# The second tile of a 31-tap convolution goes from VectorE to GpSimd, and the norm behind it runs beside the local attention

## The chip, the cores and the metric

One core of a Trainium2 chip runs the whole program. The metric is the time of one execution on the device in microseconds (us). The engines of the core are TensorE (PE; its weight loads are PEld), VectorE (DVE), ScalarE (ACT), GpSimd (POOL) and SyncE (SP), which issues the DMAs. Each engine works through its own queue strictly in order.

## The reference

Two layers of a transformer-like trunk in float32 over 512 latent tokens and 256 context tokens, width 1024. Each layer is a feed-forward block, a mixer of four parallel groups of 256 channels, and a second feed-forward block. The change is in the mixer's fourth group, the conformer convolution, and in when its norm runs:

```python
def conformer_conv_mix(z, w_conv, b_conv, g_ln, b_ln):
    a, gt = jnp.split(z, 2, axis=-1)
    u = a * jax.nn.sigmoid(gt)
    u = dw_conv(u, w_conv) + b_conv                 # 31 taps along the tokens, one weight per channel
    return jax.nn.silu(layer_norm(u, g_ln, b_ln))   # mean and variance over the 256 channels
```

The other three groups are a latent attention (4 heads, all tokens), a short gated convolution of 3 taps, and a local attention over windows of 128 tokens plus the context. All four read one input projection (`w_in`) of the normed tokens, and their outputs go through one output projection. Layer 0 computes all 768 tokens; in layer 1 the context is not needed behind its keys and values, so the convolution has 512 tokens there.

## The kernel before, in words

Activations lie with channels on the 128 partitions and tokens along the free dimension. TensorE multiplies float32 numbers that are split into a rounded high part and a rest, in three products (`mm3`, L168). Each weight tile of 128x1024 is loaded into one of four buffers `raw` (`load`, L158), taken round robin, and split in two halves of 512 columns into `wh` (ScalarE, L139) and `wl` (VectorE, L140).

`mixer` goes through these stages for each layer.

1. Two pairs of projections give the convolution's input `u`, two tiles of 128 channels (L725 writes them). Between latent and context tokens and at both ends lie 15 zero columns, so one instruction covers all tokens: 783 columns in layer 0, 512 in layer 1. `gap_conv` then makes each output tile `y` with 31 instructions: the middle tap with the bias (L651), and 30 of the form y = u shifted * w + y (L653). Both tiles run on VectorE. They are recorded at a priority of -1000 (`P_CONV`), so that the scheduler places them, when the program is built, where it expects VectorE to be free.
2. Projections of the local attention's queries, keys and values follow, with their rotations (L620 to L623) and copies for the products (L1006, L1014).
3. Local attention: per unit (`Window`, 12 units in layer 0, 8 in layer 1) scores on TensorE (L841 to L849), maximum, exponential and sum, and then GpSimd multiplies the probabilities by the reciprocal of the sum (L869). TensorE transposes them (L628 in `transposed`), and multiplies them by the values (L792, L793). The loop over `units` runs the softmax of unit i, the transposes of unit i - 1 and the products of unit i - 2. Between these it takes steps of the generator `others` (function `more`), which holds the projections of the short convolution and of the latent attention, eight steps of weights each. Their sums go to the PSUM tile `pmod` and a spare one.
4. Latent attention: the same loop goes on with 8 or 16 units of `Latent`. Here steps 4 to 7 (`CN`) each advance the generator `conformer_norm`: sums over the channels by products with a matrix of ones (L758), the subtraction of the mean (L762), the squares (L767), their sums and inverse root, the multiplication (L772), Silu with gain and shift (L775) and the split for the output projection. In this stage the buffers `raw[2]` and `raw[3]` also take weights of the modulation (L182), which a second generator, `filler`, works off.

The scheduler fixes the order of each engine's instructions when the program is built. At run time an engine waits for what its next instruction needs, and nothing behind it may pass.

Of the kernel before, what the change touches and what calls it, by code (L numbers as in the profile page):

```python
# [13 lines left out]
ALU = mybir.AluOpType  # L14
AX = mybir.AxisListType

P = 128
D = 1024
KD = D // P
# [12 lines left out]
CF_K = 31  # L32
# [14 lines left out]

class K:
    N_RAW, N_MRAW, N_W = 4, 2, 5
    CN = (4, 5, 6, 7)  # L50

    FFN_MODS = (0, range(2, 6)), (1, range(0, 4)), (1, range(4, 6)), (1, ())
    MIX_MODS = range(6, 9)
# [591 lines left out]
    def gap_conv(self, y, u, w, bias, n):  # L645
# [3 lines left out]
        for j in [mid] + [j for j in range(CF_K) if j != mid]:  # L649
            if j == mid:  # L650
                nc.vector.tensor_scalar(out=y[:, :n], in0=u[:, j:j + n], scalar1=w[:, j:j + 1], scalar2=bias, op0=ALU.mult, op1=ALU.add)  # L651
            else:
                nc.vector.scalar_tensor_tensor(out=y[:, :n], in0=u[:, j:j + n], scalar=w[:, j:j + 1], in1=y[:, :n], op0=ALU.mult, op1=ALU.add)  # L653


    def mixer(self, l, n, st):

        nc = self.nc
# [6 lines left out]
        nq = n // P  # L665
# [44 lines left out]
        dd = []  # L710
        us = []
        gap = self.GAP

        places = [(a, b, a + i * gap) for i, (a, b) in enumerate(segs)]
        for i in range(2):
            u = self.wide.popleft()
# [8 lines left out]
                    nc.vector.tensor_tensor(out=v[:, c - a:e - a], in0=ps, in1=v[:, c - a:e - a], op=ALU.mult)  # L725
            us.append(u)

        with self.rise(self.P_CONV):
            for i in range(2):
                y = self.wide.popleft()  # L730
                a, b, p = places[-1]
                self.gap_conv(y, us[i], self.vcol(l, "wcf", i * CF_K, CF_K), self.vcol(l, "bcf", i), p + b - a)
                dd.append(y)

        wq = []
# [15 lines left out]
            nc.scalar.activation(wv[:, a:b], ps, AF.Copy)  # L751

        def conformer_norm():
            self.give(*(u[:, :TOK] for u in us))
            pm = self.turn(self.dbl)
            for i, y in enumerate(dd):
                for a, b, p in places:
                    nc.tensor.matmul(pm[:, a:b], self.ones, y[:, p:p + b - a], start=i == 0, stop=i == 1)  # L758
            zs = [self.S(), self.S()]
            for y, z in zip(dd, zs):  # L760
                for a, b, p in places:
                    nc.vector.scalar_tensor_tensor(out=z[:, a:b], in0=pm[:, a:b], scalar=-1.0 / 256, in1=y[:, p:p + b - a], op0=ALU.mult, op1=ALU.add)  # L762
            self.give(*(y[:, :TOK] for y in dd))
            yield
            sqs = [self.S(), self.S()]
            for z, sq in zip(zs, sqs):
                nc.scalar.activation(sq[:, :n], z[:, :n], AF.Square)  # L767
            yield
            rl = self.inv_rms(self.turn(self.dbl), [(sq, P) for sq in sqs], n, 1.0 / 256)
            self.give(*sqs)  # L770
            for z in zs:
                nc.vector.tensor_tensor(out=z[:, :n], in0=z[:, :n], in1=rl[:, :n], op=ALU.mult)  # L772
            yield
            for i, z in enumerate(zs):
                nc.scalar.activation(z[:, :n], z[:, :n], AF.Silu, scale=self.vcol(l, "gln", i), bias=self.vcol(l, "bln", i))  # L775
            for j, t in zip((6, 7), zs):
                out(j, t)
            yield


        po = self.one
# [33 lines left out]
        so, _ = VEC["sink"]  # L815
# [207 lines left out]
        def out(i, t):  # L1023
            o[i] = self.split_new(t[:, :n], n)
            self.give(t)
# [16 lines left out]
        def others():  # L1042

            def short(i):
                t = self.turn(temps)
                for a, b, ps in (yield from slow(T_SC + 2 + i, n)):
                    nc.scalar.activation(t[:, a:b], ps[:, :b - a], AF.Copy)
                for a, b, ps in (yield from slow(T_SC + 4 + i, n)):
                    nc.vector.tensor_tensor(out=t[:, a:b], in0=ps[:, :b - a], in1=t[:, a:b], op=ALU.mult)
                cv = self.S()  # L1050
                self.dw_conv(cv, t, self.vcol(l, "wsc", i * SC_K, SC_K), SC_K, segs)
                for a, b, ps in (yield from slow(T_SC + i, n)):
                    nc.vector.tensor_tensor(out=cv[:, a:b], in0=ps[:, :b - a], in1=cv[:, a:b], op=ALU.mult)
                ob.append(cv)

            temps = deque(t[:, :TOK] for t in self.mraw)
            yield from short(0)

            pk = yield from slow(T_KV, TOK)
            ckv, sq = self.S(), self.turn(temps)  # L1060
            for a, b, ps in pk:
                nc.scalar.activation(ckv[:, a:b], ps[:, :b - a], AF.Copy)
                nc.scalar.activation(sq[:, a:b], ps[:, :b - a], AF.Square)
            for j in range(6):
                nc.tensor.matmul(spare[:, 256 + j:257 + j], sq[:, j * P:(j + 1) * P], self.ones[:, :1], start=True, stop=True)
            self.rsqrt(self.rc, spare[:, 256:262], 1.0 / 128)
            for a, b, ps in pk:
                self.spread(ps, self.rc[:, a // P:b // P])
                nc.vector.scalar_tensor_tensor(out=ckv[:, a:b], in0=ckv[:, a:b], scalar=self.vcol(l, "gkv"), in1=ps[:, :b - a], op0=ALU.mult, op1=ALU.mult)

            pq = yield from slow(T_QA, n)
            lat["kv"] = self.split_new(ckv, TOK)
            self.give(ckv)
            qa, sqa = self.S(), self.turn(temps)
            for a, b, ps in pq:
                nc.scalar.activation(sqa[:, a:b], ps[:, :b - a], AF.Square)
                nc.scalar.activation(qa[:, a:b], ps[:, :b - a], AF.Copy, scale=self.vcol(l, "gq", 0))
            lat["qa"] = self.split_new(qa[:, :n], n)
            self.give(qa)
            qw = query_weights(256)  # L1080
            pq = yield from slow(T_QB, TOK, 96)
            qb, sqb = self.S(), self.turn(temps)
            for a, b, ps in pq:
                if a < n:
                    nc.scalar.activation(sqb[lower, a:b], ps[lower, :b - a], AF.Square)
                    nc.scalar.activation(qb[lower, a:b], ps[lower, :b - a], AF.Copy, scale=self.vcol(l, "gq", 1)[lower])
                nc.scalar.activation(qb[64:96, a:b], ps[64:96, :b - a], AF.Copy)
            pr = spare[:, 256:]
            for t in range(nq):
                c = slice(t * P, (t + 1) * P)  # L1090
                nc.tensor.matmul(pr[:, 2 * t:2 * t + 2], sqa[:, c], self.ones[:, :2], start=True, stop=False)
                nc.tensor.matmul(pr[:, 2 * t:2 * t + 2], sqb[lower, c], self.ones[lower, :2], start=False, stop=True)
            rq = lat["rq"] = self.rq[l][:, :2 * nq]
            self.rsqrt(rq, pr[:, :2 * nq], 1.0 / 192)
            nc.vector.tensor_scalar(out=rq, in0=rq, scalar1=96 ** -0.5, scalar2=None, op0=ALU.mult)

            mqb = lat["qb"] = self.R()
            nc.scalar.activation(mqb[lower, :n], qb[lower, :n], AF.Copy)
            nc.vector.tensor_tensor(out=mqb[upper, :n], in0=qb[lower, :n], in1=mqb[lower, :n].bitcast(F32), op=ALU.subtract)
            self.rope(qb, 64, 96, self.cos_m, self.sin_m, self.mask_m)  # L1100
            lat["kr"] = qb

            q = lat["rot"] = self.S()
            parts = [(0, SEQ, self.mod_ps[:, :SEQ])] + ([(SEQ, n, spare[:, :n - SEQ])] if n > SEQ else [])
            mla_query(parts, 0, *qw)
            for a, b, ps in parts:
                nc.scalar.activation(q[:, a:b], ps, AF.Copy)
            self.rope(q, 0, P, self.cos_m, self.sin_m, self.mask_m, self.turn(temps))
            yield from short(1)

        units = [Window(t, kv) for kv in range(2) for t in range(nq)]
# [5 lines left out]
        cuts.close()  # L1117
        quad, spare = self.psum(cuts, 1, 1536)[0], self.psum(cuts, 1, 512)[0]
        lt, lv = self.LAGS
        cn, rest, done, total = conformer_norm(), others(), 0, 9 * KD  # L1120

        def more(share):

# [5 lines left out]
        for i in range(len(units) + lv):  # L1129
            j = i - nw  # L1130
            if j == -1:
                qw, kw = query_weights(), kv_weights()
            if j == 0:
                more(1)
                for _ in rest:
                    pass
                for t in (*x, wqs[1], wks[1]):
                    self.give(*t)
                cuts.close()
                self.dbl = self.psum(cuts, 2, 1024)  # L1140
                mraw = self.mraw
                self.mraw = deque(mraw + deque([self.raw[2], self.raw[3]]))
                self.filler = self.mod_parts(l, self.MIX_MODS)
                rot.extend(self.split_new(lat["rot"][:, :n], n))
                mla_queries(0, *qw)
                mla_keys(0, kw)
                self.give(lat["kr"], lat["rot"])
# [22 lines left out]
            if j == lv - 1:  # L1170
                self.give(*wvs)
            if j in self.CN:
                next(cn, None)
            if 0 <= j < 4:
                k, t = ((4, oc[0]), (2, ob[0]), (3, ob[1]), (5, oc[-1]))[j]
                out(k, t)
# [1 line left out]
                out(0, oa[0])  # L1178
            if j >= 0:
                self.fill(2)  # L1180
        for _ in cn:
            pass
        self.rest()
        self.mraw = mraw
        out(1, oa[1])
# [260 lines left out]
```

## Time and profile before

| | |
|---|---|
| median of 3 runs | 2645.79 us (2644.46 to 2647.66) |
| profiled execution | 2646.68 us, span of its instructions 2644.9 us |
| granted TensorE clock, mean | 0.987 |
| busy: TensorE, VectorE, ScalarE, GpSimd | 2573.0, 2173.6, 1131.2, 76.2 us |
| mixer of layer 0, local attention | about 640 to 770 us |
| mixer of layer 1, local attention | about 2032 to 2148 us |

Times are counted from the start of the span. A busy share is an average over stages with different limits, so the stretches are shown one by one below. In a line of the timeline or of a group, "[0.69 <-POOL f L869]" or the part behind the bar is the idle time of the engine before it and what ended it. Tiles go by the program's names, without buffer numbers: `f` are the mixer's float32 tiles (the convolution's inputs and outputs and the probabilities among them), `r` its rounded ones, `sm` small statistics, `ps`, `pmod` and `pone` PSUM tiles, `vec` the per-channel constants (the taps among them).

### The profile page before, as it was taken

The page shows a single profiled execution, that of the slowest core. Times are in us where ns is not written, and L with a number is a line of the kernel's source. Part 1 is how long each engine was busy: PE and PEld are TensorE (multiplying, and loading weights), DVE is VectorE, ACT ScalarE, POOL GpSimd, SP SyncE. Part 2 cuts the span into 40 slices and gives each one's busy share as a digit, 9 for nine tenths or more (in the row PEclk, how much of TensorE's full clock was granted, in tenths as well). Part 3 has the DMA queues.
Part 4 walks back from the last instruction along what each step waited for, and adds up shares of the span by engine and source line. Part 5 has one row for each costly group of instructions (what it writes and reads, how often), then busy time and mean ns, then how long its engine had stood idle before and what let it go on. Part 6 is the DMA issues. An engine that isn't in the chain of part 4 may idle for free.

```text
span 2644.9 us, 39614 instructions
## 1 busy us (share of the span) xinstructions
PE 2573.0 (97%) x15361; PEld 2430.6 (92%) x15361; DVE 2173.6 (82%) x4188; ACT 1131.2 (43%) x2118; POOL 76.2 (3%) x98
## 2 busy tenths in 40 slices
PE   7999999999998999999999999999999999999998
PEld 5999999987876999999999999999998776989998
DVE  5999987779877499999997778677679885788887
ACT  5333333444567343333324433234344565544444
POOL 0000000000212000000000000000000111000000
PEclk9999999999999999999999999999999999999999
DMA  7334332221134242344433112222121144323332
GB/s 279 125 103 130 116 99 64 80 72 34 39 124 136 64 152 88 105 136 144 125 115 96 48 60 65 68 64 80 58 85 60 43 128 129 122 85 96 96 101 76
DMA packets 78702, 257.24 MB, mean 97 GB/s; under 512 B 8753, under 2 KB 14385, under 8 KB 77873
## 3 DMA queue, kind: packets, MB, share of 16 engines
q1 hardware_dynamic: 78512, 254.70, 30.3%
q8 instruction: 120, 1.97, 0.3%
q14 instruction: 70, 0.57, 0.1%
HBM read 252.57 MB, written 2.10 MB: 96 GB/s over the span
## 4 chain that ended last, share of the span: by engine, by line
PE 65%; DVE 6%; ACT 2%; DMA 1%; issue 1%; POOL 0%; SPq 0%; DVEq 0%; ACTq 0%; POOLq 0%
PE ps L168 48%; PE pmod L168 7%; PE pone L168 5%; DVE f L653 1%; PE ps L628 1%; PE pmod L185 1%; DVE wl L140 1%; DMA raw<-in_w_mod 1%; PE pone L792 1%; DMA raw<-in_w_gu 1%; DVE r L140 1%; PE pone L793 1%; DVE f L140 0%; DVE sm L907 0%; DVE sm L855 0%
## 5 line engine op out<-in xcount | busy, mean ns | idle before, releaser
L168 PE MATMUL ps<-x,wh 128*128 128x384 f32 (+1 forms) x2888 | 703.2, 328 | 0.0
L168 PEld LDWEIGHTS ps<-x,wh 128*128 128x128 f32 x2888 | 510.8, 188 | 0.1
L168 PE MATMUL ps<-x,wl 128*128 128x384 f32 (+1 forms) x1444 | 473.1, 328 | 0.0
L139 ACT ACTIVATE wh<-raw 128x512 fp32r<-128x512 f32 (+1 forms) x439 | 275.1, 628 | 445.5 <-PE ps L168 264.2
L140 DVE TENSOR_TENSOR wl<-raw,wh 128x512 fp32r<-128x512 f32 (+1 forms) x439 | 302.0, 690 | 81.6 <-ACT wh L139 75.4
L168 PE MATMUL ps<-t,wh 128*128 128x384 f32 (+2 forms) x1408 | 364.9, 341 | 0.3 <-DVE t L140 0.3
L139 ACT ACTIVATE wh<-t 128x512 fp32r<-128x512 f32 x217 | 135.8, 629 | 328.6 <-PE ps L168 157.6
L168 PEld LDWEIGHTS ps<-x,wl 128*128 128x128 f32 x1444 | 271.2, 188 | 0.1
L323 DVE SCALAR_TENSOR_TENSOR h<-ps,hg,h 128x128 f32<-128x128 f32 (+3 forms) x376 | 174.4, 508 | 111.5 <-PE ps L168 109.9
L168 PE MATMUL ps<-r,wh 128*128 128x512 f32 (+3 forms) x1070 | 262.1, 337 | 0.4 <-DVE r L318 0.2
L168 PEld LDWEIGHTS ps<-t,wh 128*128 128x128 f32 x1408 | 254.8, 188 | 7.1 <-DVE t L140 0.5
L168 PE MATMUL ps<-t,wl 128*128 128x384 f32 (+2 forms) x704 | 239.1, 341 | 0.0
L477 DVE TENSOR_TENSOR t<-t,ps 128x384 f32<-128x384 f32 (+1 forms) x384 | 196.2, 516 | 31.0 <-PE ps L168 29.0
L139 ACT ACTIVATE t<-t 128x384 fp32r<-128x384 f32 (+2 forms) x247 | 130.0, 534 | 180.9 <-DVE t L471 72.7
L222 DVE CUSTOM_DVE_ANT_0 t<-mraw,t,vec 128x1024 bf16<-128x1024 f32 x160 | 204.7, 1280 | 3.1 <-ACT t L547 2.4
L168 PEld LDWEIGHTS ps<-r,wh 128*128 128x128 f32 (+1 forms) x1070 | 181.3, 189 | 22.4 <-DVE r L318 0.9
L168 PE MATMUL ps<-x,t 128*128 128x384 f32 (+1 forms) x1284 | 199.4, 309 | 0.0
L168 PEld LDWEIGHTS ps<-x,t 128*128 128x128 f32 x1284 | 189.7, 188 | 0.0
L140 DVE TENSOR_TENSOR wl<-t,wh 128x512 fp32r<-128x512 f32 x217 | 148.7, 688 | 36.4 <-ACT wh L139 36.2
L168 PE MATMUL ps<-r,wl 128*128 128x512 f32 (+3 forms) x535 | 170.6, 337 | 3.4 <-ACT r L317 2.8
L168 PE MATMUL ps<-t,t 128*128 128x384 f32 (+2 forms) x876 | 173.6, 346 | 0.0
L168 PEld LDWEIGHTS ps<-t,t 128*128 128x128 f32 x876 | 152.8, 188 | 9.7
(261 smaller groups left out, 4331.4 us busy)
## 6 DMA issues: line engine op xcount, KB each, us to landing
raw<-in_w_gu SPq DMA_DIRECT2D x160, 512.0 KB, 3.9
raw<-in_w_dn SPq DMA_DIRECT2D x88, 512.0 KB, 3.7
mraw<-in_w_modt SPq DMA_DIRECT2D x80, 512.0 KB, 3.7
raw<-in_w_in SPq DMA_DIRECT2D x34, 512.0 KB, 3.6
mraw<-in_w_mod SPq DMA_DIRECT2D x24, 512.0 KB, 3.8
raw<-in_w_mod SPq DMA_DIRECT2D x24, 512.0 KB, 4.6
raw<-in_w_out SPq DMA_DIRECT2D x20, 512.0 KB, 3.9
i<-in_w_mod SPq DMA_DIRECT2D x32, 256.0 KB, 6.3
```

The costliest lines, as they stand in the source:

```text
L139: self.nc.scalar.activation(hi, x, AF.Copy)
L140: self.nc.vector.tensor_tensor(out=lo, in0=x, in1=hi.bitcast(F32), op=ALU.subtract)
L168: self.nc.tensor.matmul(ps[:, c:e], a, b[:, c:e], start=start and i == 0, stop=stop and i == 2)
L185: nc.tensor.matmul(ps[32 * j:32 * j + 32, :256], self.sc[:, k, :], r[:, j * 256:(j + 1) * 256], start=k == 0, stop=k == KD - 1)
L222: self.nc.vector.tensor_tensor_reduce(out=waste, in0=r, in1=c[:, i * D:(i + 1) * D], scale=1.0, scalar=self.vcol(l, "b_mod", t), op0=ALU.m ...
L323: nc.vector.scalar_tensor_tensor(out=self.h[:, k, s:e], in0=ps[:, s - a:e - a], scalar=gate[:, k, i:i + 1], in1=self.h[:, k, s:e], op0=ALU ...
L477: eng.tensor_tensor(out=out, in0=p, in1=q, op=op)
L628: self.nc.tensor.transpose(out, in_, self.ident)
L653: nc.vector.scalar_tensor_tensor(out=y[:, :n], in0=u[:, j:j + n], scalar=w[:, j:j + 1], in1=y[:, :n], op0=ALU.mult, op1=ALU.add)
L792: nc.tensor.matmul(po[:, :256], v, p[1], start=start, stop=False)
L793: nc.tensor.matmul(po[:, :256], v, p[0], start=False, stop=stop)
```

## The change

The second output tile of the convolution is made on GpSimd, by a new function with two instructions for a tap: a scaling into a scratch tile `t`, and an add of it to `y`. The scratch tile is one of the four `raw` buffers, taken out of the ring from here to the start of the latent attention. The first tile stays on VectorE. `conformer_norm` is no longer advanced from the loop's latent steps, but runs inside `others`, between the latent attention's rotated queries and the second half of the short convolution, with the PSUM tiles `mod_ps` and `spare` that the projections there use. Steps 4 and 5 of the loop now only split the result.

```diff
-    CN = (4, 5, 6, 7)
+    CN = (4, 5)
...
+    def gap_conv_b(self, y, u, w, bias, n, t):
+
+        gp = self.nc.gpsimd
+        mid = CF_K // 2
+        for j in [mid] + [j for j in range(CF_K) if j != mid]:
+            gp.tensor_scalar(out=(y if j == mid else t)[:, :n], in0=u[:, j:j + n], scalar1=w[:, j:j + 1], scalar2=bias if j == mid else 1.0,
+                             op0=ALU.mult, op1=ALU.add if j == mid else ALU.mult)
+            if j != mid:
+                gp.tensor_tensor(out=y[:, :n], in0=y[:, :n], in1=t[:, :n], op=ALU.add)
...
+        held = self.raw.pop()
         with self.rise(self.P_CONV):
             for i in range(2):
                 y = self.wide.popleft()
                 a, b, p = places[-1]
-                self.gap_conv(y, us[i], self.vcol(l, "wcf", i * CF_K, CF_K), self.vcol(l, "bcf", i), p + b - a)
+                args = y, us[i], self.vcol(l, "wcf", i * CF_K, CF_K), self.vcol(l, "bcf", i), p + b - a
+                if i == 0:
+                    self.gap_conv(*args)
+                else:
+                    self.gap_conv_b(*args, held)
                 dd.append(y)
...
-            pm = self.turn(self.dbl)
-            for i, y in enumerate(dd):
-                for a, b, p in places:
-                    nc.tensor.matmul(pm[:, a:b], self.ones, y[:, p:p + b - a], start=i == 0, stop=i == 1)
-            zs = [self.S(), self.S()]
+            parts = [(p, a, b, ps) for (a, b, p), ps in zip(places, (self.mod_ps, spare))]
+            for p, a, b, ps in parts:
+                for i, y in enumerate(dd):
+                    nc.tensor.matmul(ps[:, :b - a], self.ones, y[:, p:p + b - a], start=i == 0, stop=i == 1)
+            zs.extend((self.S(), self.S()))
...
             self.rope(q, 0, P, self.cos_m, self.sin_m, self.mask_m, self.turn(temps))
+            yield from conformer_norm()
             yield from short(1)
...
-        cn, rest, done, total = conformer_norm(), others(), 0, 9 * KD
+        rest, done, total = others(), 0, 9 * KD + 4
...
                 self.dbl = self.psum(cuts, 2, 1024)
+                self.raw.append(held)
...
             if j in self.CN:
-                next(cn, None)
+                out(6 + self.CN.index(j), zs[self.CN.index(j)])
...
-        for _ in cn:
-            pass
```

On GpSimd in layer 0, before, the first softmax scale follows the zero columns of the convolution's inputs (`f_4838` is the second one):

```order
L718 MEMSET f_4834 128x15 x3
L718 MEMSET f_4838 128x15 x3
L869 ISA
L869 TENSOR_SCALAR f_4862<-f_4862,sm 128x512
L869 TENSOR_SCALAR f_4866<-f_4866,sm 128x512
L869 TENSOR_SCALAR f_4870<-f_4870,sm 128x640
L869 TENSOR_SCALAR f_4878<-f_4878,sm 128x640
```

The same place after the change (`f_4846` is the output tile, `raw_62` the lent buffer; at the mark 27 more pairs of a scaling and an add; the softmax scale is L890 now):

```order
L728 MEMSET f_4838 128x15 x3
L660 ISA
L660 TENSOR_SCALAR f_4846<-f_4838,vec_99 128x783
L660 TENSOR_SCALAR raw_62<-f_4838,vec_99 128x783
L663 TENSOR_TENSOR f_4846<-f_4846,raw_62 128x783
...
L890 TENSOR_SCALAR f_4862<-f_4862,sm 128x512
L890 TENSOR_SCALAR f_4866<-f_4866,sm 128x512
L660 TENSOR_SCALAR raw_62<-f_4838,vec_99 128x783
L663 TENSOR_TENSOR f_4846<-f_4846,raw_62 128x783
L890 TENSOR_SCALAR f_4870<-f_4870,sm 128x640
```

In all 30 scalings and 29 adds stand ahead of the first unit's softmax scales, and the last pair behind them. In layer 1 all 31 scalings and 30 adds stand ahead of them.

On TensorE in layer 0, before, the first transposes (L628 from `f_4862` and `f_4866`, the first unit's probabilities) come three matmuls behind the second unit's scores (L841 to L844):

```order
L841 MATMUL ps_5628<-r_4970,r_4958 128x384
L841 MATMUL ps_5628<-r_4974,r_4958 128x384
L844 MATMUL ps_5628<-masks_r,ident_r 128x128 x2
L168 MATMUL pmod<-r_4890,wl_74 128x512
L168 MATMUL pmod<-r_4894,wh_73 128x512
L168 MATMUL pmod<-r_4890,wh_73 128x512
L628 MATMUL ps_4998<-ident,f_4862 128x128
L628 MATMUL ps_5002<-ident,f_4862 128x128
```

After the change (the scores are L862 to L870 now):

```order
L862 MATMUL ps_5658<-r_4970,r_4958 128x384
L862 MATMUL ps_5658<-r_4974,r_4958 128x384
L865 MATMUL ps_5658<-masks_r,ident_r 128x128 x2
L628 MATMUL ps_4998<-ident,f_4862 128x128
L628 MATMUL ps_4998<-ident,f_4866 128x128
...
L168 MATMUL pmod<-r_4890,wl_74 128x512
L168 MATMUL pmod<-r_4894,wh_73 128x512
```

The transposes stand directly behind the scores, and the projection's matmuls, which read nothing of the softmax, behind the transposes.

## Rows read from the trace of the kernel before

**Rows 1.** The page: busy time by engine, and the chain's shares.

```profile
PE 2573.0 (97%) x15361; PEld 2430.6 (92%) x15361; DVE 2173.6 (82%) x4188; ACT 1131.2 (43%) x2118; POOL 76.2 (3%) x98
...
PE 65%; DVE 6%; ACT 2%; DMA 1%; issue 1%; POOL 0%; SPq 0%; DVEq 0%; ACTq 0%; POOLq 0%
```

**Rows 2.** Busy time by stretch (columns first): local attention, then latent attention.

```profile
core 0: us, PE busy (x) PEld busy (x) DVE busy (x) ACT busy (x) POOL busy (x), PEclk, DMA share, GB/s
640.00:770.00 130.00, 122.96 (x780) 108.11 (x779) 109.27 (x217) 74.76 (x169) 21.69 (x24) 0.96 0.16 48
2032.00:2148.00 116.00, 108.54 (x633) 89.41 (x631) 104.02 (x196) 68.63 (x140) 16.04 (x16) 0.99 0.21 61
770.00:860.00 90.00, 79.60 (x592) 61.88 (x593) 68.56 (x157) 64.60 (x122) 21.04 (x24) 0.96 0.44 150
2148.00:2220.00 72.00, 63.48 (x428) 48.95 (x426) 52.06 (x112) 52.59 (x95) 16.07 (x16) 0.90 0.36 120
```

**Rows 3.** VectorE's groups, 601.7 to 649.1 us, then 2011.8 to 2052.

```profile
L653 DVE SCALAR_TENSOR_TENSOR f<-f,vec,f 128x783 f32<-128x783 f32 x24 | 24.2, 1030 | 0.0
L140 DVE TENSOR_TENSOR wl<-raw,wh 128x512 fp32r<-128x512 f32 x11 | 7.5, 685 | 0.0
L1006 DVE TENSOR_TENSOR r<-f,r 64x768 fp32r<-64x768 f32 x4 | 3.8, 954 | 0.1
L621 DVE TENSOR_TENSOR f<-f,f 128x512 f32<-128x512 f32 x3 | 2.1, 691 | 0.0
L651 DVE TENSOR_SCALAR f<-f,vec 128x783 f32<-128x783 f32 x1 | 0.7, 682 | 0.0
...
L653 DVE SCALAR_TENSOR_TENSOR f<-f,vec,f 128x512 f32<-128x512 f32 x24 | 17.2, 747 | 0.0
L651 DVE TENSOR_SCALAR f<-f,vec 128x512 f32<-128x512 f32 x1 | 0.5, 541 | 0.0
```

**Rows 4.** Timeline of GpSimd: start, length; the first scales of each layer.

```profile
649.09 1.66 POOL L869 TENSOR_SCALAR f<-f,sm 128x512 f32<-128x512 f32 x2 [87.75 <-DVE sm L867]
...
2051.97 2.63 POOL L869 TENSOR_SCALAR f<-f,sm 128x512 f32<-128x512 f32 x2 [75.47 <-DVE sm L867]
```

**Rows 5.** TensorE's first transposes in the timeline, and waits: total, times, longest.

```profile
650.13 0.33 PE L628 MATMUL ps<-ident,f 128*128 128x128 f32 x1 [0.69 <-POOL f L869]
...
2053.56 0.33 PE L628 MATMUL ps<-ident,f 128*128 128x128 f32 x1 [0.70 <-POOL f L869]
...
PE pmod L292 <- DVE sm L858: 1.6, 1, 1.6
...
PE pmod L292 <- DVE sm L858: 1.0, 1, 1.0
```

**Rows 6.** Timeline of VectorE: the convolution's second input, layers 0 and 1.

```profile
600.71 1.02 DVE L725 TENSOR_TENSOR f<-ps,f 128x512 f32<-128x512 f32 x2
...
2011.13 0.68 DVE L725 TENSOR_TENSOR f<-ps,f 128x512 f32<-128x512 f32 x1
```

**Rows 7.** Timeline of GpSimd: scales by width, and the first one of all.

```profile
649.09 0.99 POOL L869 TENSOR_SCALAR f<-f,sm 128x512 f32<-128x512 f32 x1 [87.75 <-DVE sm L867]
...
738.01 1.37 POOL L869 TENSOR_SCALAR f<-f,sm 128x512 f32<-128x512 f32 x2 [15.12 <-DVE sm L867]
...
807.07 0.91 POOL L912 TENSOR_SCALAR f<-f,sm 128x768 f32<-128x768 f32 x1 [8.42 <-DVE sm L911]
...
813.22 0.48 POOL L912 TENSOR_SCALAR f<-f,sm 128x256 f32<-128x256 f32 x1 [2.87 <-DVE sm L911]
```

**Rows 8.** Timelines of both engines where they work at once, 656 to 673 us.

```profile
656.44 1.03 DVE L653 SCALAR_TENSOR_TENSOR f<-f,vec,f 128x783 f32<-128x783 f32 x1
656.63 1.51 POOL L869 TENSOR_SCALAR f<-f,sm 128x640 f32<-128x640 f32 x1 [5.89 <-issue]
...
664.48 0.68 DVE L1049 TENSOR_TENSOR mraw<-pmod,mraw 128x512 f32<-128x512 f32 x1
664.53 1.58 POOL L869 TENSOR_SCALAR f<-f,sm 128x640 f32<-128x640 f32 x2 [5.62 <-issue]
...
671.41 1.51 POOL L869 TENSOR_SCALAR f<-f,sm 128x512 f32<-128x512 f32 x1 [5.29 <-DVE sm L867]
672.35 1.39 DVE L653 SCALAR_TENSOR_TENSOR f<-f,vec,f 128x783 f32<-128x783 f32 x1
```

**Rows 9.** Stretches of 2 us behind a stop of TensorE (PEclk is eighth).

```profile
693.00:695.00 2.00, 0.38 (x4) 0.14 (x3) 1.98 (x5) 1.22 (x4) 0.00 (x0) 0.70 0.00 0
695.00:697.00 2.00, 2.00 (x10) 2.00 (x10) 1.81 (x5) 1.93 (x3) 0.00 (x0) 0.50 0.34 98
699.00:701.00 2.00, 2.00 (x9) 1.71 (x9) 1.94 (x4) 0.22 (x1) 2.00 (x2) 0.59 0.00 0
```

**Rows 10.** Timeline of SP: weight loads issued in the local attention, layer 0.

```profile
661.61 20.20 SPq L158 DMA_DIRECT2D raw<-in_w_in  x4
```

More of the change, by code (lines that the diff above doesn't have):

```diff
@@ L754, in conformer_norm @@
             self.give(*(u[:, :TOK] for u in us))
-            pm = self.turn(self.dbl)
-            for i, y in enumerate(dd):
-                for a, b, p in places:
-                    nc.tensor.matmul(pm[:, a:b], self.ones, y[:, p:p + b - a], start=i == 0, stop=i == 1)
-            zs = [self.S(), self.S()]
+            parts = [(p, a, b, ps) for (a, b, p), ps in zip(places, (self.mod_ps, spare))]
[3 more added lines that the diff above has]
+            zs.extend((self.S(), self.S()))
             for y, z in zip(dd, zs):
-                for a, b, p in places:
-                    nc.vector.scalar_tensor_tensor(out=z[:, a:b], in0=pm[:, a:b], scalar=-1.0 / 256, in1=y[:, p:p + b - a], op0=ALU.mult, op1=ALU.add)
+                for p, a, b, ps in parts:
+                    nc.vector.scalar_tensor_tensor(out=z[:, a:b], in0=ps[:, :b - a], scalar=-1.0 / 256, in1=y[:, p:p + b - a], op0=ALU.mult, op1=ALU.add)
             self.give(*(y[:, :TOK] for y in dd))
@@ L768, in conformer_norm @@
             yield
-            rl = self.inv_rms(self.turn(self.dbl), [(sq, P) for sq in sqs], n, 1.0 / 256)
+            for j in range(nq):
+                for i, sq in enumerate(sqs):
+                    nc.tensor.matmul(spare[:, 256 + j:257 + j], sq[:, j * P:(j + 1) * P], self.ones[:, :1], start=i == 0, stop=i == 1)
             self.give(*sqs)
-            for z in zs:
-                nc.vector.tensor_tensor(out=z[:, :n], in0=z[:, :n], in1=rl[:, :n], op=ALU.mult)
+            self.rsqrt(self.rc[:, :nq], spare[:, 256:256 + nq], 1.0 / 256)
+            for p, a, b, ps in parts:
+                self.spread(ps, self.rc[:, a // P:b // P])
+                for z in zs:
+                    nc.vector.tensor_tensor(out=z[:, a:b], in0=z[:, a:b], in1=ps[:, :b - a], op=ALU.mult)
             yield
@@ L775, in conformer_norm @@
                 nc.scalar.activation(z[:, :n], z[:, :n], AF.Silu, scale=self.vcol(l, "gln", i), bias=self.vcol(l, "bln", i))
-            for j, t in zip((6, 7), zs):
-                out(j, t)
             yield
+        zs = []
         po = self.one
```

## The prediction, made before the changed kernel ran

> **What bounds the kernel now.** I read the page first. TensorE's matmul records cover 97% of the 2644.9 us span and VectorE is busy 82%, GpSimd 3%; the chain of work that ended last is 65% TensorE [rows 1]. So time is won or lost only where TensorE stands still or runs at half clock. Second view: busy time by stretch, for the local attention (640 to 770 us in layer 0, 2032 to 2148 in layer 1) and the latent attention behind it. TensorE is short of full by 7.0 and 7.5 us in the two local stretches and by 10.4 and 8.5 us in the two latent ones [rows 2]. All that a lighter VectorE can bring in the mixer lies in these 33 us. Third view: the grouped instructions of VectorE between the arrival of the convolution's second input and the first softmax scale. VectorE is full there, with 24 taps in each layer [rows 3]. Fourth view: GpSimd in order of time. Its first work after the pads is the scaling of the first unit's probabilities, at 649.09 us in layer 0 and 2051.97 in layer 1, after 87.75 us of waiting in layer 0 [rows 4]. TensorE's first transposes (L628) wait for that scale, 0.69 and 0.70 us today [rows 5].
>
> **What is moved.** Per layer 31 VectorE instructions of the second tile go to GpSimd as 31 scalings and 30 adds. The two listings of order show what matters: on GpSimd, which works strictly in that order, 30 scalings and 29 adds stand ahead of the first L890 scale in layer 0, and all 61 in layer 1. On TensorE the first transposes stand where they stood, right behind the second unit's scores, with the local attention's projections queued behind them. So the first scale now waits for GpSimd's convolution, L628 waits for the scale, and all of TensorE waits for L628.
>
> **When GpSimd gets there, layer 0.** It can start when the second input is written: L725 starts at 600.71 and its two pieces take 1.02, so 601.7 [rows 6]. A scaling has the same form as the softmax scale, which undisturbed takes 0.91 us at 768 columns, 0.48 at 256, and 1.37 for two, or 0.69 each, at 512 [rows 7]. That is 0.84 ns a column on a fixed 0.27; at 783 columns 0.92. The add with two inputs is nowhere in this trace on GpSimd. Its lower bound is the one-input time, 0.92; its upper bound two of them, 1.84. I take 0.27 + 2 x 0.66 = 1.58, the column part twice, because the next rows show GpSimd and VectorE taking turns at reading SBUF, as two inputs of one GpSimd instruction then would. Own time: 30 x 0.92 + 29 x 1.58 = 73.4 us.
>
> The Trainium skill (GPSIMD Engine Reference, section 3.1, "Elementwise — side-by-side cycle accounting") gives 4497 ns for such an add of 2048 columns; an estimate in proportion is 1.72 us at 783 columns and 1.12 at 512, with which the whole sum would come out 4 us higher. No run here shows that figure yet.
>
> Then the turns. A 640-column scale takes 0.79 us (two in 1.58 at 664.53) beside a VectorE multiply with one input in PSUM (664.48), but 1.51 when a VectorE tap began just ahead of it at 656.44; a 512-column one takes 1.51 at 671.41 behind two weight splits, and a tap begun behind it (672.35) 1.39 instead of 1.03 [rows 7, 8]. So an instruction of VectorE with both inputs in SBUF and one of GpSimd exclude each other. Each meeting cost GpSimd 0.7 to 0.8 here, and 0.3 at 649.09 (0.99 against 0.69) [rows 7, 8]. In the new order of VectorE I count 46 instructions of that kind between the second input and the first unit's reciprocal: 19 taps of the first tile, 10 splits, 9 of the rotations and 8 of 64x768, all with rows of the old stretch [rows 3]. GpSimd's fixed 0.27 can run beside such an instruction, so one costs it its record less 0.27: 0.76 for a tap, 0.42 for a 512-column one, 0.68 at 64x768; records of successive VectorE instructions overlap by about 0.1, so I take 0.5 each (bounds 0.3 and 0.8, as measured), 23 us. GpSimd reaches the first scale at 601.7 + 73.4 + 23.0 = 698.1 instead of 649.09: 49.0 us late.
>
> The Trainium skill (SBUF — State Buffer, section "Who interferes with whom") speaks against the change: it says that the port pair which the two engines share is an exclusive lock, and that whichever starts second stands still for the whole of the other's instruction. Rows 8 agree.
>
> **Layer 1** has 512 columns: 0.69 and 0.27 + 2 x 0.43 = 1.13 us (bounds 0.69 and 1.38). 31 x 0.69 + 30 x 1.13 = 55.3 us; 48 meetings (21 taps, 10 splits, 9, 8) with shorter instructions (0.75 against 1.03 a tap [rows 3]) at 0.4, so 19.2. Start 2011.13 + 0.68 = 2011.8 [rows 6]; first scale at 2086.3 instead of 2051.97: 34.3 us late.
>
> **What hides it.** Nothing on TensorE: its queue is in order and the next matmuls stand behind L628. Before that point VectorE, which must itself wait its turn, delivers the weight splits late, but TensorE's lost time there ends at the same L628, so I don't add it.
>
> **The other edits.** VectorE loses 31 instructions a layer (30 x 1.03 + 0.68 = 31.6 us and 30 x 0.75 + 0.54 = 23.0 of busy time [rows 3]). What of it frees TensorE is part of the 7.0 + 7.5 us missing in the local stretches [rows 2], between nothing and all; I take half, -7. A stall halves the clock: after the 1.6 us stop at 693 us the granted clock was 0.50, 1.2 GHz, from 695 to 699 and back at 1.00 by 701 [rows 9], about 6 us at half speed or 3 us lost (693 to 701: shares 0.70, 0.50, 0.50, 0.59 of 2 us each, 3.4 us). I add 3 for each of the two new stalls, +6; bounds 0 and 8. The conformer's norm moves from the latent to the local attention with as many matmuls; at the new place the matmuls of a projection stand behind its two chains (sums, then squares, root and spread). Such a chain stands there today, the latent key's, and TensorE waits 1.6 and 1.0 us for its spread (L292) [rows 5]. I add 2 a layer, +4; bounds 0 and two waits of 1.6 a layer, 6.4. One weight buffer of four is lent: the next SP load into it (a modulation weight) waits for the last tap, and in layer 0 five loads stand behind it. They start at 661.61 today [rows 10], with the delay of 49 at about 710, by when the tap is done: nothing. If the tap were later than that, SP's delay would be TensorE's.
>
> **Sum.** 49.0 + 34.3 - 7 + 6 + 4 = 86.3. The profiled execution took 2646.68 us (span 2644.9 and 1.8 around it), so 2733.0 by its own time; the median of the three runs is 0.9 lower, 2645.79, so 2732 us.
>
> **Bounds.** Low: adds at 0.92 and 0.70, meetings at 0.3 and 0.25: 54.3 + 13.8 = 68.1 and 42.7 + 12 = 54.7 us, so 20.7 and 14.5 us late, less 14 of relief: +21, 2667. High: adds at 1.84 and 1.38, meetings at 0.8 and 0.6: 27.6 + 53.4 + 36.8 = 117.8 and 62.8 + 28.8 = 91.6, so 70.4 and 51.4 late, with 8 for the clock, 6.4 for the norm and no relief: +136, 2782.
>
> **Rivals.** *Faster: GpSimd keeps up.* If an instruction of its convolution took under (649.09 - 601.7) / 59 = 0.80 us in layer 0 and (2051.97 - 2011.8) / 61 = 0.66 in layer 1, waiting included, L628 would be no later than now, and the relief of 7 us, with some of the latent stretches' 19, would be left: with 3 of these 2636. For it speaks that GpSimd is idle 97% of the span. Against it: one-input instructions alone take 0.92 and 0.69.
>
> *No change.* Adds at the one-input price and no exclusion: 601.7 + 54.3 = 656.0 and 2011.8 + 42.1 = 2053.9, 6.9 and 1.9 late, less 7: 2647. Rows 8 show the exclusion, which leaves this little.
>
> *GpSimd loses nearly every turn* while VectorE has work. It then starts in earnest when VectorE is through its own work before the first scale: the old stretch of 47.4 us less five taps and a scaling (5.8), so 643.3 in layer 0, and 40.2 less three taps and a scaling (2.8), so 2049.2 in layer 1. With 73.4 and 55.3 more the scales are 67.6 and 52.5 us late: 2769 with the other terms. The row at 671.41, where it waited behind two splits, is for it; 1.51 at 656.63, behind one tap, against.
>
> *VectorE is the late one.* With turns about it gets one instruction in for each of GpSimd's, and what L628's successors need (weight splits, the next unit's maxima) comes after GpSimd is done, by up to as long again as the turns cost GpSimd, 23 and 19 us: 2755 to 2774. Against it: its 46 instructions meet 59 of GpSimd's.
>
> **Chances.** Forecast (GpSimd's queue delays the first scale by 35 to 65 us and 22 to 48 us) 0.74; GpSimd losing its turns 0.12; VectorE late 0.06; no change 0.05; faster 0.03. The measurement can tell about 0.2%, 5 us, from no change. Slower 0.92, same 0.05, faster 0.03. Range 2680 to 2785: the forecast's own and most of the two slower rivals.
>
> **What would show it.** Right: one GpSimd group of 61 two-input and one-input instructions per layer with next to no idle time between; taps of the first tile on VectorE well over 1.03 us; one TensorE wait of tens of us at the first L628 of each layer, released by L890, and a half clock behind it; stretches outside the mixer unchanged. Wrong: GpSimd's adds at 0.9 us or less, or an L628 that starts by 655 and 2057 us.

## The result, and the profile after

The changed kernel takes 2754.3 us (median of 4 runs, 2753.6 to 2755.3), beside 2646.7 for the kernel before on the same chip: a ratio of 1.041, 95% interval 1.040 to 1.042. The forecast of 2732 us had the direction and the wait that ends last, and the range of 2680 to 2785 holds the time; the lateness of the first scales was 25 us too small, and what VectorE loses was told in it as a detail. The span grew by 106.9 us, from 2644.9 to 2751.8.

First the page after, busy time by engine, as in [rows 1].

```profile
PE 2586.0 (94%) x15361; PEld 2440.7 (89%) x15361; DVE 2186.5 (79%) x4128; ACT 1126.1 (41%) x2114; POOL 257.4 (9%) x220
```

VectorE has 60 records fewer, and is still busier than before, 2186.5 against 2173.6 us. A busy share alone would not tell why; the groups of VectorE from 602 to 682 us in layer 0 do (count, busy time, mean ns).

```profile
L653 DVE SCALAR_TENSOR_TENSOR f<-f,vec,f 128x783 f32<-128x783 f32 x19 | 33.7, 1774 | 0.3
L140 DVE TENSOR_TENSOR wl<-raw,wh 128x512 fp32r<-128x512 f32 x10 | 15.6, 1559 | 0.0
L1027 DVE TENSOR_TENSOR r<-f,r 64x768 fp32r<-64x768 f32 x4 | 8.1, 2032 | 0.1
L621 DVE TENSOR_TENSOR f<-f,f 128x512 f32<-128x512 f32 x3 | 3.7, 1224 | 0.0
L876 DVE TENSOR_REDUCE sm<-ps 128x1 f32<-128x512 f32 x2 | 1.3, 678 | 0.0
L140 DVE TENSOR_TENSOR r<-ps,r 128x384 fp32r<-128x384 f32 x2 | 1.1, 546 | 0.0
```

Against [rows 3] a tap takes 1.774 us instead of 1.030, a weight split 1.559 instead of 0.685, a copy of 64x768 2.032 instead of 0.954, a rotation's product 1.224 instead of 0.691. All these have both inputs in SBUF. The last two rows read PSUM, and took no longer than in that stretch of before:

```profile
L855 DVE TENSOR_REDUCE sm<-ps 128x1 f32<-128x512 f32 x2 | 1.3, 684 | 0.0
L140 DVE TENSOR_TENSOR r<-ps,r 128x384 fp32r<-128x384 f32 x2 | 1.1, 550 | 0.0
```

All of VectorE's work from 602 to 682 us would take some 45 us at the means of before; beside GpSimd it takes the 80 us.

Now GpSimd. First its groups over the whole span, then its timeline: a pair (a scaling and its add) beside VectorE, a pair of each layer when VectorE has nothing to do, the last add of layer 0 ahead of the scales, and the first scales.

```profile
L663 POOL TENSOR_TENSOR f<-f,raw 128x783 f32<-128x783 f32 x30 | 65.3, 2178 | 2.5
L663 POOL TENSOR_TENSOR f<-f,raw 128x512 f32<-128x512 f32 x30 | 44.9, 1496 | 2.5
L660 POOL TENSOR_SCALAR raw<-f,vec 128x783 f32<-128x783 f32 x30 | 41.1, 1371 | 2.8
```

```profile
653.83 1.77 POOL L660 TENSOR_SCALAR raw<-f,vec 128x783 f32<-128x783 f32 x1
655.68 2.43 POOL L663 TENSOR_TENSOR f<-f,raw 128x783 f32<-128x783 f32 x1
...
689.24 0.93 POOL L660 TENSOR_SCALAR raw<-f,vec 128x783 f32<-128x783 f32 x1
690.26 1.83 POOL L663 TENSOR_TENSOR f<-f,raw 128x783 f32<-128x783 f32 x1
...
710.87 1.83 POOL L663 TENSOR_TENSOR f<-f,raw 128x783 f32<-128x783 f32 x1
712.68 1.36 POOL L890 TENSOR_SCALAR f<-f,sm 128x512 f32<-128x512 f32 x2
...
2148.03 0.69 POOL L660 TENSOR_SCALAR raw<-f,vec 128x512 f32<-128x512 f32 x1
2148.80 1.26 POOL L663 TENSOR_TENSOR f<-f,raw 128x512 f32<-128x512 f32 x1
...
2164.97 1.36 POOL L890 TENSOR_SCALAR f<-f,sm 128x512 f32<-128x512 f32 x2
```

The undisturbed prices are 0.93 and 1.83 us (0.69 and 1.26 in layer 1), and between one instruction and the next, which needs its output or the scratch tile that it reads, lie 0.09 to 0.10 us: 689.24 + 0.93 ends 0.09 before 690.26. The first scale starts at 712.68 instead of 649.09, 63.6 us late. In layer 1 it is 85.9 us behind the start of the L735 that writes the second input (2079.07) instead of 40.8 behind L725 [rows 4, 6], 45.1 late.

TensorE's idle time for this falls into several pieces. Here are its waits of 600 to 780 us, then of 2070 to 2260 (total, times, longest), and behind them the stretches of layer 0 (busy columns as in [rows 2]; the eighth figure is the granted clock).

```profile
PE ps L628 <- POOL f L890: 28.0, 2, 27.9
PE ps L628 <- ACT f L766: 27.8, 1, 27.8
PE ps L862 <- DVE r L140: 4.6, 1, 4.6
PE ps L862 <- ACT f L883: 2.6, 1, 2.6
...
PE ps L628 <- POOL f L890: 25.4, 2, 25.2
PE ps L628 <- ACT f L766: 13.6, 1, 13.6
```

Before, the wait for ScalarE's copy (L751 there, L766 now) was this, in layer 0:

```profile
PE ps L628 <- ACT f L751: 0.7, 1, 0.7
```

The stretches of layer 0 after the change:

```profile
600.00:640.00 40.00, 34.92 (x197) 29.75 (x195) 39.69 (x31) 8.77 (x15) 36.58 (x19) 1.00 0.10 31
640.00:660.00 20.00, 0.00 (x0) 0.00 (x0) 19.87 (x15) 3.65 (x6) 19.15 (x10) 0.50 0.09 27
660.00:680.00 20.00, 12.50 (x57) 11.14 (x58) 19.93 (x15) 4.97 (x8) 19.11 (x10) 0.74 0.11 30
680.00:720.00 40.00, 9.31 (x42) 8.01 (x41) 7.54 (x14) 7.05 (x16) 35.66 (x27) 0.57 0.05 14
720.00:770.00 50.00, 48.76 (x317) 43.38 (x316) 27.76 (x72) 25.39 (x64) 8.00 (x12) 1.00 0.13 43
```

So the delay has two halves. From 635 to 680 VectorE is full and TensorE waits for what VectorE owes; from 684 on VectorE is all but idle and TensorE waits for GpSimd's queue. The first half looks like ScalarE's doing (L766), but ScalarE's and VectorE's timelines show who holds it up:

```profile
658.75 0.84 ACT L1032 ACTIVATE r<-f 64x768 fp32r<-64x768 f32 x1 [16.28 <-DVE f L623]
...
662.09 0.79 ACT L766 ACTIVATE f<-ps 128x768 f32<-128x768 f32 x1
...
683.98 0.17 DVE L888 RECIPROCAL sm<-sm 128x2 f32<-128x2 f32 x1
```

ScalarE stood 16.28 us for a rotation (L623) that VectorE had not finished, with the copy of the values (L766) behind it in its queue, and TensorE's transposes of these values behind that. And VectorE's reciprocal (L888) ended at 684.15: with an empty GpSimd queue the first scale would have started there, 35.1 us late. GpSimd's queue added the 28.5 to 712.68.

What follows is nearly as long as before. Below, two stretches before and the same two after: from the first scale of each layer to the first add of its output projection.

```profile
649.10:873.50 224.40, 208.98 (x1406) 177.00 (x1405) 172.23 (x363) 138.03 (x284) 42.72 (x48) 0.96 0.27 88
2052.00:2238.30 186.30, 171.40 (x1075) 135.13 (x1075) 140.49 (x285) 113.85 (x223) 32.08 (x32) 0.95 0.32 100
```

```profile
712.70:939.86 227.16, 214.98 (x1407) 180.70 (x1408) 147.10 (x338) 135.98 (x282) 39.95 (x51) 0.95 0.27 87
2165.00:2345.60 180.60, 168.44 (x1069) 133.23 (x1070) 119.58 (x254) 108.55 (x219) 30.79 (x32) 0.95 0.32 104
```

Together 407.8 instead of 410.7 us: VectorE has 46 us less to do there, and that bought 3. The sum of the whole: 63.6 + 45.1 for the first scales, 2.8 and -5.7 for these stretches, 1.6 for the stretch between the mixers (939.86 to 2079.07 against 873.51 to 2011.13) and -0.4 behind the second make 107.0, of 106.9.

### The profile page after: what moved, and what is told of

Its sections match the earlier page's. It is cut to its first block, busy times and chain, and to the rows that moved or that the text cites. A ratio compares the mean times of both kernels' runs of the same rounds, so it can differ in the third digit from the quotient of the medians.

```text
span 2751.8 us, 39683 instructions
## 1 busy us (share of the span) xinstructions
PE 2586.0 (94%) x15361; PEld 2440.7 (89%) x15361; DVE 2186.5 (79%) x4128; ACT 1126.1 (41%) x2114; POOL 257.4 (9%) x220
## 5 line engine op out<-in xcount | busy, mean ns | idle before, releaser
L140 DVE TENSOR_TENSOR wl<-raw,wh 128x512 fp32r<-128x512 f32 (+1 forms) x439 | 314.5, 718 | 90.7 <-ACT wh L139 87.8
L323 DVE SCALAR_TENSOR_TENSOR h<-ps,hg,h 128x128 f32<-128x128 f32 (+3 forms) x376 | 174.5, 509 | 112.5 <-PE ps L168 110.8
```

The lines of the kernel that those rows point to most:

```text
L140: self.nc.vector.tensor_tensor(out=lo, in0=x, in1=hi.bitcast(F32), op=ALU.subtract)
L323: nc.vector.scalar_tensor_tensor(out=self.h[:, k, s:e], in0=ps[:, s - a:e - a], scalar=gate[:, k, i:i + 1], in1=self.h[:, k, s:e], op0=ALU ...
```

## The experiments

The question behind the right sign: is the loss GpSimd's queue, as the forecast had it, or VectorE's slower pace, and what does the norm's new place cost? Times are medians, with the ratio to the kernel before on the same chip and its interval; not all runs were on one chip, and the ratios go across.

**The norm alone.**

```diff
-                if i == 0:
-                    self.gap_conv(*args)
-                else:
-                    self.gap_conv_b(*args, held)
+                self.gap_conv(*args)
```

> The norm's move alone: both tiles' taps stay on VectorE, the norm runs beside the local attention, and one raw buffer is held as in the change. Theory (the time goes to GpSimd's convolution, the norm's place costs about nothing): in the profile of after the local stretch of layer 0 is some 14 us longer beyond the late first scale and that of layer 1 some 9, and the latent stretches give 12.6 and 12.0 back; so 2647 us within 10, the first scale still at about 649 us. Rival (a good part of the 107 us is the norm, whose matmuls stand in TensorE's queue and wait for taps and for VectorE's chain): 2665 us or more, with a wait of several us at L774.

Measured: 2639.7 us, 0.9984 (0.9975 to 0.9994). The first scale is at 649.19, in layer 1 at 2055.10. The norm beside the local attention costs nothing; alone it is a gain of about 4 us. The rival falls.

**The convolution alone.** The kernel before, with `gap_conv_b` and the return of `held` as in the diff of the change, and the norm where it was.

```diff
+        held = self.raw.pop()
...
-                self.gap_conv(y, us[i], self.vcol(l, "wcf", i * CF_K, CF_K), self.vcol(l, "bcf", i), p + b - a)
+                args = y, us[i], self.vcol(l, "wcf", i * CF_K, CF_K), self.vcol(l, "bcf", i), p + b - a
+                if i == 0:
+                    self.gap_conv(*args)
+                else:
+                    self.gap_conv_b(*args, held)
```

> The convolution's move alone: the second tile on GpSimd with the scratch buffer, the norm in the latent attention as before. Theory: the first scales are as late as in the changed kernel (63.6 and 45 us), and the time is within 10 us of its 2754. Rival (norm): under 2735 us, the difference to 2754 being the norm's part.

Measured: 2751.3 us, 1.0405 (1.0387 to 1.0423), with the waits of the changed kernel: at L628 27.9 us for GpSimd and 27.7 for ScalarE. The whole loss, within these intervals, is the convolution's move.

**The scales out of GpSimd's queue.**

```diff
-                    nc.gpsimd.tensor_scalar(out=w.prs[g][:, :wide], in0=w.prs[g][:, :wide], scalar1=sm[:, g:g + 1], scalar2=1.0,
-                                            op0=ALU.mult, op1=ALU.mult)
+                    nc.scalar.activation(w.prs[g][:, :wide], w.prs[g][:, :wide], AF.Copy, scale=sm[:, g:g + 1])
```

> The changed kernel with the local attention's softmax scales on ScalarE, so that they no longer stand behind the convolution in GpSimd's queue. Theory of two bounds (the scale waits for GpSimd's queue, but VectorE, which does in 80 us beside GpSimd what took it 46 us before, would itself have been ready only at about 683 us in layer 0 against 649 before, and at 70 us behind the second input against 40 in layer 1): first scale at about 684 us and 70 us behind the second input, some 28 and 15 us gained, 2711 to 2725 us. Rival A (queue order alone): nothing is late without the queue, 2650 to 2665 us. Rival B (VectorE gets next to nothing until GpSimd is through): first scale at about 711 us still, 2745 us or more.

Measured: 2727.2 us, 1.0312 (1.0293 to 1.0331). ScalarE's timeline at the first scales, and TensorE's largest wait in layer 0:

```profile
683.54 1.34 ACT L890 ACTIVATE f<-f,sm 128x512 f32<-128x512 f32 x2 [0.61 <-DVE sm L888]
...
2118.41 1.33 ACT L890 ACTIVATE f<-f,sm 128x512 f32<-128x512 f32 x2 [1.69 <-DVE sm L888]
```

```profile
PE ps L628 <- ACT f L766: 27.8, 1, 27.8
```

The wait for L890 is gone, and the first scale starts at 683.54, as the theory of two bounds said (684), released by VectorE's reciprocal. In layer 1 it is 60.4 behind L735 (2058.01), nearer than the 70 expected. So the first scales are still 34.5 and 19.6 us later than before, 54 us without any queue. Yet the time is 2 us above the top of that theory's range: of the 80.8 us that the span is longer than before, the other 27 lie behind the first scales, 12.5 in layer 0 (683.54 to 920.47, where the first add of the output projection starts, 236.9 us for 224.4) and 14.4 in layer 1 (2118.41 to 2319.08, 200.7 for 186.3). In layer 0 GpSimd works on beside VectorE; the stretch of 700 to 720 us of this run has TensorE busy for 14.33 us, VectorE 18.00 and GpSimd 16.37:

```profile
700.00:720.00 20.00, 14.33 (x81) 12.49 (x82) 18.00 (x31) 8.00 (x22) 16.37 (x11) 0.91 0.08 26
```

In layer 1 the largest of these losses is not VectorE's pace, but the lent buffer. SP stands for the convolution's last add before it may load into that buffer (L182), with the load of weights for the latent attention's queries (`in_w_uqb`) behind it in its queue; ScalarE stands for these weights, and a split that TensorE's next transposes wait for stands behind. SP's wait, the load behind it, ScalarE's wait and TensorE's (8.3 us the longest), in this order:

```profile
SPq L182 <- POOL f L663: 39.8, 1, 39.8
...
2146.56 1.13 SPq L996 DMA_DIRECT2D raw<-in_w_uqb  x2
...
2151.21 0.31 ACT L1000 ACTIVATE wl<-raw 64x128 fp32r<-64x128 f32 x1 [15.82 <-DMA raw<-in_w_uqb]
...
PE ps L628 <- DVE f L140: 10.1, 4, 8.3
```

Rival A, the queue alone, misses by 62 us, rival B by 18.

**Its control: the kernel before with the same edit.**

> The kernel before, with only the local attention's softmax scales on ScalarE: the control for the run with the changed kernel's scales there, which was 2727 us. If ScalarE's extra work costs nothing, 2640 to 2650 us, and the 80 us that were left in that run belong to GpSimd's convolution beside VectorE. If ScalarE is the bound of the local attention, up to 40 scales x 0.72 = 29 us more, 2660 to 2675, and only some 55 of the 80 belong to the convolution.

Measured: 2640.9 us, 0.9987 (0.9977 to 0.9997). ScalarE's extra work costs nothing, so the convolution on GpSimd costs 2727.2 - 2640.9 = 86 us (the same by the ratios, 1.0312 and 0.9987) even where no softmax scale waits behind it. Taking the scales out of the queue gives back only some 27 of the 107 us. The 54 us of late first scales are VectorE's slower pace; what of the rest is, and what the lent buffer's, is not separated beyond the 8.3 us wait.

**Half the taps on GpSimd.** 16 of the 31, the others left out.

```diff
-        for j in [mid] + [j for j in range(CF_K) if j != mid]:
+        for j in [mid] + list(range(15)):
             gp.tensor_scalar(
```

> The changed kernel with 16 of the 31 taps of the second tile (the other 15 are left out of the computation). Theory of two bounds: GpSimd would be through with the 15 pairs ahead of the first scale at about 602 + 110.8 x 31/59 = 660 us, but VectorE, at 46/80 of its pace until then, at about 602 + 58 + (46 - 33) = 673; first scale at 670 to 676 us, 24 late, in layer 1 some 14 late, 2680 to 2692 us. Rival A (GpSimd's queue alone): first scale at 660 and 2 us late in layer 1, 2655 to 2665 us. Rival B (the time has little to do with how many taps GpSimd makes): over 2735 us.

Measured: 2689.9 us, 1.0172 (1.0148 to 1.0195), with no wait for L890 among TensorE's and the 27.8 us for L766 as before:

```profile
663.91 2.45 POOL L663 TENSOR_TENSOR f<-f,raw 128x783 f32<-128x783 f32 x1
...
678.91 1.37 POOL L890 TENSOR_SCALAR f<-f,sm 128x512 f32<-128x512 f32 x2 [12.55 <-ACT mraw L1068]
```

GpSimd ends its last add at 666.36 and stands idle for 12.55 us until the first scale is wanted, 30 us late. The releaser named is ScalarE; what GpSimd lacked was the softmax, behind VectorE's work. Rival A (660 us, 2655 to 2665) falls; the scale came 3 us behind the theory's window, the time in its range.

**Few taps left on VectorE.** 3 of the first tile's 31, the others left out; GpSimd has its whole convolution.

```diff
-        for j in [mid] + [j for j in range(CF_K) if j != mid]:
+        for j in [mid, 0, 1]:
             if j == mid:
```

> The changed kernel with 3 of the 31 taps of the first tile on VectorE (the other 28 are left out of the computation), so that GpSimd meets fewer VectorE instructions. Theory (GpSimd's own pace of 0.93 and 1.83 us and 0.09 between, and some 0.4 us for each meeting): 28 scalings and 27 adds stand ahead of the first scale, 80.4 us own, some 27 meetings left, 11 us: first scale at 693 us against 712.7; in layer 1 own 64.7 + 7, at 72 us behind the second input against 85; 2708 to 2730 us. Rival (GpSimd's records beside VectorE are its own time, no meetings): first scale at 705 us or later, over 2740 us.

Measured: 2724.5 us, 1.0302 (1.0288 to 1.0316). Its GpSimd groups of layer 0 and TensorE's two largest waits there:

```profile
L663 POOL TENSOR_TENSOR f<-f,raw 128x783 f32<-128x783 f32 x30 | 60.2, 2006 | 2.4
L660 POOL TENSOR_SCALAR raw<-f,vec 128x783 f32<-128x783 f32 x30 | 35.3, 1176 | 2.8
```

```profile
PE ps L628 <- POOL f L890: 35.4, 2, 35.2
PE ps L628 <- ACT f L766: 9.4, 1, 9.4
```

The same GpSimd instructions are shorter with less on VectorE (2.006 and 1.176 us against 2.178 and 1.371 on the mean), and the first scale starts at 696.34 (693 expected, 712.7 in the changed kernel), in layer 1 at 76.6 behind GpSimd's start (72 expected, 85.05 in the changed kernel). Of the 16.3 us in layer 0 some 4.9 come from the order, in which one scaling and two adds fewer stand ahead of the scale here; in layer 1 the order is the same. The rival, that the long records are GpSimd's own, falls. And the weight shifts: with 19 taps fewer beside GpSimd on VectorE, of the 46 instructions that the prediction counted, the wait for L766 shrinks to 9.4 us and the queue's grows to 35.2. GpSimd's own pace is enough to hold TensorE back.

**A small share.** 6 of the second tile's taps on GpSimd, the other 25 behind them on VectorE (`first` lets `gap_conv` skip the middle tap and those below it); the whole computation.

```diff
-        for j in [mid] + [j for j in range(CF_K) if j != mid]:
+        for j in [mid] + list(range(5)):
             gp.tensor_scalar(
...
                     self.gap_conv_b(*args, held)
+                    self.gap_conv(*args, first=5)
```

> A small share for GpSimd, the whole computation: 6 of the second tile's 31 taps on GpSimd (11 instructions), the other 25 behind them on VectorE, the norm beside the local attention. Theory (each pair takes GpSimd some 4.2 us, in which VectorE gets through only 46/80 of its work and so loses 1.8 us, more than the 1.03 of the tap that it is spared): GpSimd is through at about 627 us, long before the first scale, VectorE 10 us late there and 6 of it made up later: 2645 to 2657 us. Rival (only the queue matters, and a share that GpSimd finishes in time is a gain): 2630 to 2639 us.

Measured: 2658.7 us, 1.0050 (1.0036 to 1.0064), 2 us above the theory's range. The first scale is at 662.34, 13 us late (10 expected), after 37.85 us in which GpSimd was idle:

```profile
662.34 1.65 POOL L893 TENSOR_SCALAR f<-f,sm 128x512 f32<-128x512 f32 x2 [37.85 <-DVE sm L891]
```

So a share that GpSimd finishes long before it is due loses too. By number of taps on GpSimd the times are 2640 (none), 2659 (6), 2690 (16, with 15 left out) and 2754 (31): some 3 us a tap in both layers together up to 16, and some 4 from there to 31, where the queue comes on top. The steps are not quite alike: with 6, VectorE keeps the other 25 of that tile.

**The norm alone, with all four weight buffers.** As the first experiment, without `held`.

```diff
-        held = self.raw.pop()
...
-                self.raw.append(held)
```

> The norm's move alone with all four raw buffers in the ring (both tiles on VectorE). If the ring of three made TensorE wait for weights in the local attention, the first scale of layer 1, 3.2 us later than before in the run with three, comes back and the time is 2633 to 2638 us; if not, as that run, 2640 within 4.

Measured: 2641.0 us, 0.9979 (0.9970 to 0.9987). The layer 1 scale is back at 2052.61, but the time differs from the first experiment's by less than either's interval. It is faster than the kernel before by 0.1 to 0.3%.

**The norm early and the scales on ScalarE.** That kernel with the edit of the third experiment.

> Nothing on GpSimd beside VectorE in the local attention: the norm's move alone with four raw buffers (5 us under the kernel before by its run), and the softmax scales on ScalarE (5 us under by theirs). If the two gains are of different time, they add up: 2634 to 2638 us. If both are the same few us of VectorE time in the local attention of layer 1, which each brought forward by some 6 us alone, 2639 to 2642 us.

Measured: 2643.3 us, 0.9992 (0.9983 to 1.0001): above both expectations. The two small gains don't add up, and I have not found what takes them back; the intervals of the three runs overlap, so part of it may be scatter.

## Why the prediction was right, and what it had too small

*What is moved, and who waits for whom:* right. The first L628 of the softmax waited for L890 (27.9 and 25.2 us), L890 for the convolution ahead of it, and half the clock was granted meanwhile.

*The start and the scaling:* right. 601.88 for 601.7; 0.93 and 0.69 us for 0.92 and 0.69.

*GpSimd's own time:* this is the term that was mis-sized. The add took 1.83 us instead of 1.58 and 1.26 instead of 1.13: in layer 0 the upper bound, two one-input instructions. And I counted no time between instructions that wait for each other, some 0.09 us each, 57 times in layer 0 (5.2 us in all) and 59 in layer 1 (5.4). With both, layer 0 makes 30 x 0.93 + 29 x 1.83 + 5.2 = 86.2 instead of 73.4, and layer 1 31 x 0.69 + 30 x 1.26 + 5.4 = 64.6 instead of 55.3. That is 22.1 of the 25.4 us that were missing. The estimate from the Trainium skill (GPSIMD Engine Reference, section 3.1), 1.72 and 1.12 us an add, was nearer at 783 columns and as short at 512; the measured 1.83 and 1.26 decide.

*The turns:* right in size. From 601.88 to 712.68 are 110.8 us, less 86.2 is 24.6, for 23.0; in layer 1 from 2079.92 to 2164.97 are 85.05, less 64.6 is 20.5, for 19.2. The sentence from the Trainium skill (SBUF — State Buffer, section "Who interferes with whom"), that the engine which starts second waits out the other's instruction, agrees with both sides: GpSimd's pairs beside VectorE take 4.2 us instead of 2.94 (with the pauses), and VectorE's taps 1.774 instead of 1.030.

*"TensorE's lost time there ends at the same L628, so I don't add it":* right in the sum, and a wrong picture of the cause. VectorE's delay was not a detail under GpSimd's: it would have set the first scale 35 us late without any queue (the scales on ScalarE), sets it 30 us late with half the taps, and 13 with six. I had said that VectorE must wait its turn, but priced each meeting on GpSimd alone. And TensorE's first long wait of each layer, for the values that ScalarE copies late (L766, 27.8 and 13.6 us), stands in none of the forecast's terms or signs. The rival of VectorE as the late one had this part, but put it behind GpSimd's end, where VectorE has been all but idle since 684 us. As forecast, the queue ended last.

*Relief, clock and norm:* -7, +6 and +4 were +3 together; the stretches behind the first scales gave -2.9, with a granted clock of 0.95 in both, against 0.96 and 0.95. The norm's +4 was of the wrong sign alone (0.9984), and not to be told from zero beside the convolution on GpSimd (2751.3 and 2754.3). *The lent buffer:* nothing, as said: SP's load into it was issued at 716.93, right behind the last add (715.03 + 1.87), and none of TensorE's waits in the two stretches is for a DMA. The condition that the prediction named, a last tap that comes later than what needs the loads, was met with the scales on ScalarE, and there SP's delay did become TensorE's, 8.3 us in layer 1.

The forecast's sum with the measured own times is 86.3 + 22.1 = 108.4, of 106.9.

## What to carry to other kernels

An engine that is idle 97% of the time is no free capacity if it takes its turns at the same memory as the engine to be relieved: price each moved instruction on both engines, and count what else stands in the idle engine's queue. Where two delays end at one wait, removing the later one shows the earlier, and a buffer lent to the slow work can be the next; the time that VectorE takes for the same work before and after finds it in the profile without a run. A split in two steps through a scratch tile costs the second pass and a pause at each dependence, here 2.94 us a tap for 1.03.

## What the runs showed of the hardware

- From 602 to 682 us, beside GpSimd, VectorE's instructions with both inputs in SBUF grew (a weight split from 0.69 to 1.56 us on the mean); a maximum over 512 PSUM columns took 0.678 us, a split of 384 from PSUM 0.546, and a shuffle with one input in SBUF 0.737, all as before. Two inputs are not the whole condition: with the scales on ScalarE, a multiplication by a column of constants (L640, 256 columns, one such input) took 1.96 us beside GpSimd, and 0.34 in the kernel before.
- An add of two SBUF tiles on GpSimd cost about what two one-input instructions do: 1.83 us at 783 columns (two scalings 1.86) and 1.26 at 512 (1.38), alone; beside VectorE up to 2.49.
- With 28 of the first tile's 31 taps left out, 19 of which VectorE had run beside GpSimd, the first scale of layer 0 came forward by only 16 us, 5 of them by the order: what GpSimd needs on its own remained.
